# Branch tiles of the last stage loaded one by one, its first products in two halves of rows, and the sample columns split by GpSimd

## The chip, the core and the metric

The kernel runs on one core of one Trainium2 chip. The metric is the device time of one execution in microseconds (us). TensorE (PE) multiplies matrices into PSUM banks, VectorE (DVE) and ScalarE (ACT) work element by element and read the banks out, GpSimd (POOL) does a few small operations, and SyncE (SP) issues every DMA transfer from one queue, in order.

## What is computed

One layer of a decoder trunk for a prompt of 1024 rows and 32 sample rows (8 sequences of 4 tokens). The part that matters here is the merge at the end: two branches, each projected down to 1024 features, are gated, added, and go through the output projection.

```python
hc = head_rmsnorm(hc, mlstm_norm_w).reshape(B, S, MLSTM_WIDTH).astype(x.dtype)
bm = (hc * jax.nn.silu(m_z)) @ w_mlstm_down          # 2048 -> 1024
g_a, g_b = jnp.split(jax.nn.sigmoid(gate_pre), 2, axis=-1)
x = x + (g_a * a + g_b * bm) @ w_out
```

All matrix products keep fp32 accuracy by splitting both operands into a high and a low part and multiplying three times (high by high, low by high, high by low).

## The kernel before

Activations lie feature-major: 128 features on the partitions, the 1056 rows (1024 prompt, 32 sample) along the free axis. The columns are stored in two halves of 528, each with 512 prompt rows and then 16 sample rows. A product of 128 output features takes three PSUM banks of 352 columns, and for each bank 8 blocks of 128 input features, three matmuls each: 24 matmuls of 352 columns a bank. `fm` issues these for one weight slice `f`, and its consumer reads each bank out when it is full.

The order that counts runs through three pieces of `run`:

- `merge_gates` makes the two gates, 8 groups of 256 features, and stores each sigmoid tile `sz` in memory (`sgD`). Groups 0 to 5 run beside other work. Groups 6 and 7 run last, in the pool `gates3`. In the same stretch the last steps of the sample's recurrence run: loads of its state `ct`, products `num` and `kv`, and at the end the tile `hcS` (tag `ks`) with the sample's 32 columns of the mLSTM branch. PSUM holds two banks of the tag `mm` here, so the third product of a chain waits until ScalarE has read out the first.
- Between group 6 and group 7, `hc_tiles` loads the first four feature blocks of the branch (`hcD`, 512 KB each) into buffers with the tag `sz`, of which there are two, shared with the gates, and splits each into a high part (ScalarE, `mvhA`) and a low part (VectorE, `mvlA`).
- `downs` is the last stage but two. It loads blocks 4 to 7 into `mvhB`/`mvlB` (slot B1) and blocks 8 to 11 (slot B2) through two buffers `draw`, adds the sample's columns to each tile by `hc_sample` (ScalarE and VectorE), and multiplies: `half` 0 takes blocks 0 to 7, `half` 1 blocks 8 to 15. Now there are six `mm` banks. ScalarE reads the first half's banks out into `bm`; VectorE adds the second half's.

The text is written as one program, and a scheduler puts each engine's instructions in the order in which its own estimate of times has them ready. So the order on an engine is not the order of the text: it already opens six banks at once at the start of `downs` and puts the products of a late tile behind those of the tiles that are there. Each engine then works through its list strictly in order, and waits where an operand or a buffer is not ready.

In the rows, `wraw`, `whi` and `wlo` are a weight slice as loaded and its two parts. L391 to L393 are the three matmuls of `mm3`, L378 and L384 the two halves of a split without a scale, L380 and L386 those with one, L1332 the read-out of a gate bank, L1395 that of a `downs` bank, L1358 the loads of `hcD`, L1181 and L1191 loads and stores of the sample's state.

Of the kernel before, what the change touches and what calls it, by code (L numbers as in the profile page):

```python
# [10 lines left out]
F32 = mybir.dt.float32  # L11
F32R = mybir.dt.float32r
AF = mybir.ActivationFunctionType
ALU = mybir.AluOpType
# [4 lines left out]
P = 128  # L19
D = 1024  # L20
T = 1024
DB, DS = 8, 4
NS = DB * DS
NT = T + NS
# [5 lines left out]
CW = NT // 3  # L30
# [310 lines left out]
class Trunk:  # L341
# [103 lines left out]
    def fm(self, w, f, mov, consume, cw=CW):  # L445

        kt = len(w)
        for j in range(NT // cw):
            ps = self.mmps()
            for k in range(kt):  # L450
                wh, wl = w[k][:2]
                mh, ml = mov[k]
                s = slice(j * cw, (j + 1) * cw)
                self.mm3(ps[:, :cw], wh[:, f * P:(f + 1) * P], wl[:, f * P:(f + 1) * P], mh[:, s], ml[:, s],
                         k == 0, k == kt - 1)
            consume(j, ps)
        if kt == KT:
            self.tick()

    def feed(self, gen, rate):  # L460

        self.bg, self.rate, self.acc = gen, rate, 0.0
# [851 lines left out]
            for b in range(DB):  # L1314
                nc.sync.dma_start(O["new_pool_sample"][b, PH - DS:, s], st[PH + b * DS:PH + (b + 1) * DS, :])

    def merge_gates(self, groups):
        nc, I = self.nc, self.I
        for gg in groups:
            x, g = gg // 4, gg % 4  # L1320
            w = self.load_w(I["w_in"][:, O_GA + gg * 256:O_GA + (gg + 1) * 256], 256)
            for f in range(2):
                z = self.t(self.pp, [P, NT], "sz", bufs=2)

                plain = self.stats

                def ev(j, ps, z=z, plain=plain):
                    s = slice(j * CW, (j + 1) * CW)
                    if plain:
                        nc.scalar.activation(z[:, s], ps[:, :CW], AF.Copy)  # L1330
                    else:
                        nc.scalar.activation(z[:, s], ps[:, :CW], AF.Sigmoid)  # L1332
                self.fm(w, f, self.hmov, ev)
                if plain:
                    nc.scalar.activation(z, z, AF.Sigmoid)
                nc.sync.dma_start(self.sgD[x][g * 2 + f], z)


    def split(self, raw, slot, n=NT):
# [10 lines left out]

        return x.rearrange("p (a n) -> p a n", a=2)[:, :, part]

    def hc_tiles(self, pool, k0, slot, tag="draw"):

        out = []
        for k in range(k0, k0 + 4):
            raw = self.t(pool, [P, NT], tag, bufs=2)
            self.nc.sync.dma_start(self.halves(raw), self.hcD[k // 4][:, k % 4, :].rearrange("p (a n) -> p a n", a=2))  # L1358
            out.append(self.split(raw, slot, T))
        return out  # L1360

    def hc_sample(self, tiles, k0):
        for k, (hi, lo) in enumerate(tiles, k0):
            raw = self.hcS[:, k // 4, k % 4, :].rearrange("p (a n) -> p a n", a=2)
            s = slice(HT, HH)
            self.hi(self.halves(hi, s), raw)
            self.lo(self.halves(lo, s), raw, self.halves(hi, s))

    def downs(self, first):
        nc, I = self.nc, self.I  # L1370
        e = self.ep
        bm = [self.t(e, [P, NT], f"bm{f}") for f in range(KT)]
        movs = [first + self.hc_tiles(e, 4, "B1"), None]
        self.hc_sample(movs[0], 0)
        for half in range(2):
            mov = movs[half]
            if half == 0:
                movs[1] = self.hc_tiles(e, 8, "B2")
            else:
                mov += self.hc_tiles(e, 12, "B1")  # L1380
                self.hc_sample(mov, 8)
            for g in range(4):
                w = self.load_w(I["w_mlstm_down"][half * D:(half + 1) * D, g * 256:(g + 1) * 256], 256,
                                scale=self.mnw[:, half * 8:half * 8 + 8])
                for f in range(2):
                    ft = g * 2 + f
                    sb = None
                    if half:
                        sb = self.t(e, [P, NT], "sg", bufs=2)
                        nc.sync.dma_start(sb, self.sgD[1][ft])  # L1390

                    def ev(j, ps, ft=ft, half=half, sb=sb):
                        s = slice(j * CW, (j + 1) * CW)
                        if half == 0:
                            nc.scalar.activation(bm[ft][:, s], ps[:, :CW], AF.Copy)  # L1395
                            return
                        nc.vector.tensor_tensor(out=bm[ft][:, s], in0=ps[:, :CW], in1=bm[ft][:, s], op=ALU.add)
                        nc.vector.tensor_tensor(out=bm[ft][:, s], in0=bm[ft][:, s], in1=sb[:, s], op=ALU.mult)
                    self.fm(w, f, mov, ev)
        mov = []  # L1400
        for k in range(KT):
            raw = self.t(e, [P, NT], "draw", bufs=2)
            nc.sync.dma_start(raw, self.actD[k])
            mov.append(self.split(raw, "A" if k < 4 else "B2"))
        self.mmov = []
        self.ms = self.t(self.cp, [P, KT, NS], "qs")
        for g in range(4):
            w = self.load_w(I["w_pool_down"][:, g * 256:(g + 1) * 256], 256)
            for f in range(2):
                ft = g * 2 + f  # L1410
                sa = self.t(e, [P, NT], "sg", bufs=2)
                nc.sync.dma_start(sa, self.sgD[0][ft])

                def ev(j, ps, ft=ft, sa=sa):
                    s = slice(j * CW, (j + 1) * CW)
                    nc.vector.tensor_tensor(out=sa[:, s], in0=ps[:, :CW], in1=sa[:, s], op=ALU.mult)
                    nc.vector.tensor_tensor(out=bm[ft][:, s], in0=bm[ft][:, s], in1=sa[:, s], op=ALU.add)
                self.fm(w, f, mov, ev)
                nc.gpsimd.tensor_copy(self.ms[:, ft, :].rearrange("p (a n) -> p a n", a=2),
                                      self.halves(bm[ft], slice(HT, HH)))  # L1420
                self.mmov.append(self.split(bm[ft], "B1" if ft < 4 else "B2"))
# [151 lines left out]
    def run(self):  # L1573
# [80 lines left out]
        _p.close()  # L1654
        self.mpA, _ma = self.pool("movA")
        self.pp, _p = self.pool("gates3")
        self.merge_gates(range(6, 7))
        first = self.hc_tiles(self.pp, 0, "A", "sz")
        self.merge_gates(range(7, 8))
        self.drain()  # L1660
        _s[0].close()
        _p.close()
# [39 lines left out]
```

## Time and profile before

| | |
|---|---|
| time of three runs | 2196.43, 2198.58 (median), 2200.07 us |
| the profiled execution | 2201.45 us, span of the trace 2199.7 us |
| mean granted TensorE clock | 0.994 of full speed |
| PE busy | 2145.5 us, 98% of the span |
| DVE, ACT, POOL busy | 58%, 41%, 6% of the span |

Times in the trace count from the start of the span. The two groups of gates and the start of `downs` lie between about 1618 and 1712 us. A granted clock of 1.00 is 2.4 GHz, 0.50 is 1.2 GHz.

### The profile page before, as it was taken

To read this page: it belongs to the slowest core of one execution; us is meant where nothing else is said; L and a number is where in the kernel's file an instruction comes from. 1 tells how busy PE (TensorE), PEld (TensorE's weight loads), DVE (VectorE), ACT (ScalarE), POOL (GpSimd) and SP (SyncE) were. 2 spreads that over 40 slices of the span, in tenths; PEclk is the share of its full clock that TensorE was granted. 3 is DMA by queue.
4 is the path that set the end of the run, shared out by engine and by line. 5 is a ranking of instruction groups with operands and counts; after the bars stand their busy time and mean duration, and the time that the engine had idled before them with its cause. 6 is when DMAs were issued, how large, how long until landed. Compare 5 with 4: busy or idle time off the path is not lost.

```text
span 2199.7 us, 40300 instructions
## 1 busy us (share of the span) xinstructions
PE 2145.5 (98%) x16407; PEld 2051.3 (93%) x16407; DVE 1268.3 (58%) x2223; ACT 905.8 (41%) x1801; POOL 124.5 (6%) x335
## 2 busy tenths in 40 slices
PE   7999999999999999999999999999998999999998
PEld 6899999999999999899999998888888999999998
DVE  6856476556655575446566775765752243543654
ACT  5635454444544463544333443322332331213444
POOL 1200000000100010000000000000000000000000
PEclk9999999999999999999999999999999999999999
DMA  4233333333233322484655645877785242322112
GB/s 156 77 110 117 99 99 102 100 102 114 82 109 116 109 89 70 133 291 151 200 168 181 216 133 202 277 275 255 280 272 177 89 144 88 127 107 80 54 49 85
DMA packets 238858, 312.73 MB, mean 142 GB/s; under 512 B 14250, under 2 KB 170322, under 8 KB 238672
## 3 DMA queue, kind: packets, MB, share of 16 engines
q1 hardware_dynamic: 238672, 310.15, 43.5%
q8 instruction: 129, 2.11, 0.4%
q14 instruction: 57, 0.47, 0.1%
HBM read 200.01 MB, written 110.45 MB: 141 GB/s over the span
## 4 chain that ended last, share of the span: by engine, by line
PE 89%; DMA 4%; DVE 2%; ACT 2%; SPq 1%; issue 1%; POOL 0%; POOLq 0%; ACTq 0%; DVEq 0%
PE mm L221 22%; PE mm L163 15%; PE mm L391 12%; PE mm L392 12%; PE mm L393 12%; PE misc L962 2%; PE num L1183 2%; PE num L392 1%; PE num L393 1%; PE num L391 1%; PE kv L391 1%; PE kv L392 1%; PE kv L393 1%; PE kv L1187 1%; DMA ct<-state_mlstm_C 1%; PE misc L744 1%
## 5 line engine op out<-in xcount | busy, mean ns | idle before, releaser
L391 PE MATMUL mm<-hh,whi 128*128 128x352 f32 (+1 forms) x832 | 263.8, 317 | 13.1 <-ACT sz L1332 7.5
L392 PE MATMUL mm<-hl,whi 128*128 128x352 f32 (+1 forms) x832 | 262.6, 316 | 0.0
L393 PE MATMUL mm<-hh,wlo 128*128 128x352 f32 (+1 forms) x832 | 262.5, 316 | 0.0
L221 PE MATMUL mm<-wlo,hh 128*128 128x256 f32 x768 | 216.1, 281 | 0.0
L221 PE MATMUL mm<-whi,hl 128*128 128x256 f32 x768 | 216.1, 281 | 0.0
L221 PE MATMUL mm<-whi,hh 128*128 128x256 f32 x768 | 214.8, 280 | 0.0
L384 DVE TENSOR_TENSOR wlo<-wrawx,whi 128x1024 fp32r<-128x1024 f32 (+1 forms) x116 | 124.1, 1070 | 127.2 <-ACT whi L378 126.4
L391 PEld LDWEIGHTS mm<-hh,whi 128*128 128x128 f32 x832 | 158.8, 191 | 24.8 <-ACT sz L1332 8.6
L378 ACT ACTIVATE whi<-wrawx 128x1024 fp32r<-128x1024 f32 (+1 forms) x116 | 108.7, 937 | 174.8 <-PE mm L163 69.8
L378 ACT ACTIVATE whi<-wraw 128x1024 fp32r<-128x1024 f32 (+1 forms) x104 | 100.3, 965 | 174.5 <-PE mm L392 87.0
L384 DVE TENSOR_TENSOR wlo<-wraw,whi 128x1024 fp32r<-128x1024 f32 (+1 forms) x104 | 114.7, 1103 | 90.7 <-ACT whi L378 88.6
L393 PEld LDWEIGHTS mm<-hh,wlo 128*128 128x128 f32 x832 | 158.7, 191 | 8.3 <-issue 6.7
L392 PEld LDWEIGHTS mm<-hl,whi 128*128 128x128 f32 x832 | 158.7, 191 | 3.8 <-issue 2.5
L323 DVE SCALAR_TENSOR_TENSOR z<-z,vcols,z 128x556 f32<-128x556 f32 x192 | 146.4, 793 | 6.2 <-ACT z L321 4.4
L163 PE MATMUL mm<-hh,whi 128*128 128x264 f32 x512 | 148.4, 290 | 1.0 <-DVE z L179 0.6
L163 PE MATMUL mm<-hl,whi 128*128 128x264 f32 x512 | 146.1, 285 | 0.4 <-DVE hl L384 0.3
L163 PE MATMUL mm<-hh,wlo 128*128 128x264 f32 x512 | 145.5, 284 | 0.0
L221 PEld LDWEIGHTS mm<-whi,hh 128*128 128x128 f32 x768 | 144.7, 188 | 0.0
L221 PEld LDWEIGHTS mm<-whi,hl 128*128 128x128 f32 x768 | 144.6, 188 | 0.0
L221 PEld LDWEIGHTS mm<-wlo,hh 128*128 128x128 f32 x768 | 144.4, 188 | 0.2
L1188 DVE SCALAR_TENSOR_TENSOR ct<-ct,dec,kv 128x512 f32<-128x512 f32 x128 | 92.4, 744 | 85.1 <-PE kv L1187 82.5
L392 PE MATMUL mm<-mvlB,whi 128*128 128x352 f32 x384 | 123.3, 323 | 0.0
(493 smaller groups left out, 6304.3 us busy)
## 6 DMA issues: line engine op xcount, KB each, us to landing
ct<-state_mlstm_C SPq DMA_DIRECT2D x32, 1024.0 KB
new_C_sample<-ct SPq DMA_DIRECT2D x32, 1024.0 KB
wraw<-w_in SPq DMA_DIRECT2D x56, 512.0 KB
wrawx<-w_in SPq DMA_DIRECT2D x56, 512.0 KB
qkD<-z SPq DMA_DIRECT2D x64, 256.0 KB
qk<-qkD SPq DMA_DIRECT2D x16, 1024.0 KB
sgD<-sz SPq DMA_DIRECT2D x16, 528.0 KB
sg<-sgD SPq DMA_DIRECT2D x16, 528.0 KB
```

The costliest lines, as they stand in the source:

```text
L163: self.tr.nc.tensor.matmul(ps[:, j, :CH], lhsT=st[:, k], rhs=mv[k][:, c], start=start and k == 0 and n == 0, stop=stop and k == 3 and n == ...
L221: self.tr.nc.tensor.matmul(ps[:, t // 2, t % 2 * 256:t % 2 * 256 + 256], lhsT=st[k][:, c], rhs=mv[:, k], start=start and t % 2 == 0 and k ...
L323: nc.vector.scalar_tensor_tensor(out=acc, in0=z[:, o:o + tot], scalar=wc(o), in1=acc, op0=ALU.mult, op1=ALU.add)
L378: self.nc.scalar.activation(out, in_, AF.Copy)
L384: self.nc.vector.tensor_tensor(out=out, in0=in_, in1=hi.bitcast(F32), op=ALU.subtract)
L391: mm(ps, lhsT=sh, rhs=mh, start=start, stop=False)
L392: mm(ps, lhsT=sh, rhs=ml, start=False, stop=False)
L393: mm(ps, lhsT=sl, rhs=mh, start=False, stop=stop)
L744: self.nc.tensor.matmul(ps[g, f * 256:(f + 1) * 256], lhsT=self.hs[:, k, :], rhs=raw[k // 4][f][:, k % 4, :], start=k < 4, stop=k >= 4)
L962: nc.tensor.matmul(out, lhsT=qk[:, 4 + d, i * L:(i + 1) * L], rhs=qk[:, d, i * L:], start=d == 0, stop=d == 3)
L1183: nc.tensor.matmul(num[0][32 * d:32 * d + 32], lhsT=qm[:, b * P + d * NS:b * P + (d + 1) * NS], rhs=ct[:, d, :], start=b == 0, stop=b == D ...
L1188: nc.vector.scalar_tensor_tensor(out=ct[:, d, :], in0=ct[:, d, :], scalar=self.dec[:, h * DB + b, 1:2], in1=kv, op0=ALU.mult, op1=ALU.add)
```

## The change

It has four parts. `merge_gates` gets a generator to step after each gate tile and a third `sz` buffer; `hc_tiles` becomes the generator `hc_parts`, which loads a tile at each step and splits the one before it, so that the four first tiles are loaded one ahead of group 6 and one after each gate tile. In `downs` the tiles of slot B2 are loaded the same way, one step after each `fm` of the first half's groups 1 to 3. The first group of the first half goes through `fm_halves`, which opens all six banks with blocks 0 to 3 and comes back to each with blocks 4 to 7. And `hc_sample` does its two operations on GpSimd.

```diff
+    def fm_halves(self, w, mov, consume):
+
+        banks = [[self.mmps() for _ in range(3)] for _ in range(2)]
+        for k0 in (0, 4):
+            for f in range(2):
+                for j, ps in enumerate(banks[f]):
+                    s = slice(j * CW, (j + 1) * CW)
+                    for k in range(k0, k0 + 4):
+                        wh, wl = w[k][:2]
+                        mh, ml = mov[k]
+                        self.mm3(ps[:, :CW], wh[:, f * P:(f + 1) * P], wl[:, f * P:(f + 1) * P], mh[:, s], ml[:, s],
+                                 k == 0, k == 7)
+                    if k0:
+                        consume[f](j, ps)
...
-    def merge_gates(self, groups):
+    def merge_gates(self, groups, beside=None, bufs=2):
...
-                z = self.t(self.pp, [P, NT], "sz", bufs=2)
+                z = self.t(self.pp, [P, NT], "sz", bufs=bufs)
...
                 nc.sync.dma_start(self.sgD[x][g * 2 + f], z)
+                if beside is not None:
+                    next(beside)
...
+    def hc_parts(self, out, pool, k0, slot, tag="draw", bufs=2):
+
+        last = None
+        for k in range(k0, k0 + 5):
+            if last is not None:
+                out.append(self.split(last, slot, T))
+            if k == k0 + 4:
+                break
+            last = self.t(pool, [P, NT], tag, bufs=bufs)
+            self.nc.sync.dma_start(self.halves(last), self.hcD[k // 4][:, k % 4, :].rearrange("p (a n) -> p a n", a=2))
+            yield True
+        yield True
...
-            self.hi(self.halves(hi, s), raw)
-            self.lo(self.halves(lo, s), raw, self.halves(hi, s))
+            self.nc.gpsimd.tensor_copy(self.halves(hi, s), raw)
+            self.nc.gpsimd.tensor_tensor(out=self.halves(lo, s), in0=raw, in1=self.halves(hi, s).bitcast(F32),
+                                         op=ALU.subtract)
...
             if half == 0:
-                movs[1] = self.hc_tiles(e, 8, "B2")
+                movs[1] = []
+                parts = self.hc_parts(movs[1], e, 8, "B2")
...
-                    self.fm(w, f, mov, ev)
+                    if half or g:
+                        self.fm(w, f, mov, ev)
+                        if half == 0:
+                            next(parts, None)
+                    else:
+                        evs.append(ev)
+                if evs:
+                    self.fm_halves(w, mov, evs)
...
-        self.merge_gates(range(6, 7))
-        first = self.hc_tiles(self.pp, 0, "A", "sz")
-        self.merge_gates(range(7, 8))
+        first = []
+        parts = self.hc_parts(first, self.pp, 0, "A", "sz", 3)
+        next(parts)
+        self.merge_gates(range(6, 8), parts, 3)
```

Because a scheduler sets the order, the text alone does not say where an instruction ends up. Up to the last gates all engines' orders are the same. The lines of the changed text stand 15 or more further down (L1332 is L1347 there, L1358 is L1386, L1395 is L1426).

SyncE's queue in the last gates, before: `ct` is the sample's state, `sz<-hcD` are the four branch tiles, and `new_C_sample`, `sgD` are stores.

```order
L412 DMA wraw_19062<-w_mlstm_down 128x4x256
L1181 DMA ct_18652<-state_mlstm_C 128x4x512
L1191 DMA new_C_sample<-ct_18424 128x4x512
L1336 DMA sgD_44_103<-sz_18550 128x1056
L1199 DMA voz_18754<-vSD_80 128x512
L1199 DMA voz_18756<-oSD_81 128x512
L1358 DMA sz_18781<-hcD_17_76 128x2x512
...
L1336 DMA sgD_45_104<-sz_18672 128x1056
L1191 DMA new_C_sample<-ct_18652 128x4x512
L412 DMA wraw_19242<-w_mlstm_down 128x4x256
L1358 DMA sz_18793<-hcD_17_76 128x2x512
L1358 DMA sz_18799<-hcD_17_76 128x2x512
```

And in the change:

```order
L412 DMA wraw_19038<-w_mlstm_down 128x4x256
L1386 DMA sz_18538<-hcD_17_76 128x2x512
L1386 DMA sz_18678<-hcD_17_76 128x2x512
L1196 DMA ct_18654<-state_mlstm_C 128x4x512
L1206 DMA new_C_sample<-ct_18424 128x4x512
L1351 DMA sgD_44_103<-sz_18552 128x1056
L1386 DMA sz_18793<-hcD_17_76 128x2x512
...
L1351 DMA sgD_45_104<-sz_18680 128x1056
L1206 DMA new_C_sample<-ct_18654 128x4x512
L412 DMA wraw_19218<-w_mlstm_down 128x4x256
L1386 DMA sz_18891<-hcD_17_76 128x2x512
```

The first two branch tiles moved ahead of the last load of the state, and only one is left behind the last weight load, where two stood.

ScalarE's list in the last gates, before, from the second branch tile on (`voz,sss` is a step of the sample's end, `mvhA<-ks` are its columns, `sz<-mm` read-outs of gate banks):

```order
L378 ACTIVATE mvhA_18789<-sz_18787 128x2x512
L1205 ACTIVATE voz_18756,sss_18763<-shc_18761 128x512
L378 ACTIVATE mvhA_18783<-ks_18775 128x2x16
L378 ACTIVATE mvhA_18789<-ks_18775 128x2x16
L378 ACTIVATE mvhA_18795<-ks_18775 128x2x16
L378 ACTIVATE mvhA_18795<-sz_18793 128x2x512
L378 ACTIVATE mvhA_18801<-ks_18775 128x2x16
L378 ACTIVATE mvhA_18801<-sz_18799 128x2x512
L1332 ACTIVATE sz_18817<-mm_18818 128x352
L1332 ACTIVATE sz_18817<-mm_18844 128x352
L1332 ACTIVATE sz_18817<-mm_18870 128x352
```

And in the change, in the same place:

```order
L1347 ACTIVATE sz_18807<-mm_18808 128x352
L1220 ACTIVATE voz_18764,sss_18771<-shc_18769 128x512
L1347 ACTIVATE sz_18807<-mm_18834 128x352
L378 ACTIVATE mvhA_18973<-sz_18891 128x2x512
L1347 ACTIVATE sz_18807<-mm_18860 128x352
L1347 ACTIVATE sz_18893<-mm_18894 128x352
L1347 ACTIVATE sz_18893<-mm_18920 128x352
```

Two tiles and the sample's columns stood ahead of the read-out of group 7's first bank; now one tile stands ahead of its third bank, and the columns are gone from this list.

ScalarE's list at the start of `downs`, before (`draw` are the loaded tiles of slots B1 and B2, `bm<-mm` the read-outs of the six first banks):

```order
L378 ACTIVATE mvhB_2661_19012<-draw_19010 128x2x512
L378 ACTIVATE mvhB_2664_19018<-ks_18775 128x2x16
L378 ACTIVATE mvhB_2664_19018<-draw_19016 128x2x512
L380 ACTIVATE whi_19256<-wraw_19254,vcols_122 128x256 x4
L378 ACTIVATE mvhB_2667_19040<-draw_19038 128x2x512
L378 ACTIVATE mvhB_2670_19046<-ks_18775 128x2x16
L378 ACTIVATE mvhB_2670_19046<-draw_19044 128x2x512
L378 ACTIVATE mvhB_2673_19052<-ks_18775 128x2x16
L1395 ACTIVATE bm_2646_18990<-mm_19086 128x352
```

And in the change:

```order
L380 ACTIVATE whi_19232<-wraw_19230,vcols_122 128x256 x4
L378 ACTIVATE mvhB_2661_19012<-draw_19010 128x2x512
L378 ACTIVATE mvhB_2664_19018<-draw_19016 128x2x512
L378 ACTIVATE mvhB_2691_19400<-draw_19320 128x2x512
L378 ACTIVATE mvhB_2703_19508<-draw_19404 128x2x512
L1426 ACTIVATE bm_2646_18990<-mm_19062 128x352
```

The weight slice moved ahead of the third tile and the sample's columns are gone; two tiles of slot B2 still stand ahead of the first read-out.

## Rows read from the trace of the kernel before

**Rows 1.** The page's first part: busy time of each engine.
```profile
PE 2145.5 (98%) x16407; PEld 2051.3 (93%) x16407; DVE 1268.3 (58%) x2223; ACT 905.8 (41%) x1801; POOL 124.5 (6%) x335
```

**Rows 2.** Waits of PE in the whole span: us in total, times, longest us.
```profile
PE mm L391 <- ACT sz L1332: 7.5, 1, 7.5
...
PE mm L391 <- ACT bm L1395: 3.2, 1, 3.2
```

**Rows 3.** The chain that ended last, 1640 to 1725 us: start us, us, what.
```profile
1645.87 8.25 DMA sgD<-sz
...
1654.14 6.38 DMA sz<-hcD
...
1660.55 1.06 ACT mvhA L378
...
1662.18 0.66 PE mm L391
...
1666.64 0.16 PE mm L393
```

**Rows 4.** Stretches: us, busy time of each engine, granted clock, DMA share, GB/s.
```profile
1618.00:1626.00 8.00, 8.00 (x49) 7.82 (x48) 2.88 (x4) 2.94 (x4) 0.00 (x0) 1.00 0.98 309
1654.00:1662.00 8.00, 0.66 (x6) 0.40 (x4) 2.84 (x10) 3.04 (x7) 0.00 (x0) 0.85 0.54 203
1662.00:1666.00 4.00, 3.82 (x13) 3.83 (x14) 0.86 (x1) 0.48 (x2) 0.00 (x0) 0.50 0.00 0
1707.00:1711.00 4.00, 3.53 (x12) 3.53 (x13) 2.79 (x6) 4.00 (x12) 0.00 (x0) 0.57 0.61 191
```

**Rows 5.** The DMA queue SP in order of time: start us, us, transfer, count.
```profile
1626.32 0.37 SPq L1181 DMA_DIRECT2D ct<-state_mlstm_C  x1
...
1650.41 4.09 SPq L1358 DMA_DIRECT2D sz<-hcD  x2
...
1701.68 0.37 SPq L412 DMA_DIRECT2D wraw<-w_mlstm_down  x1
```

**Rows 6.** ScalarE in order of time: start us, us, operation, idle before and releaser.
```profile
1619.13 1.28 ACT L1332 ACT_TABLE_LOAD   x1 [3.12 <-DMA actD<-sz]
...
1655.03 0.47 ACT L378 ACTIVATE mvhA<-ks 128x32 fp32r<-128x32 f32 x3 [6.24 <-DVE ks L1213]
...
1702.79 1.06 ACT L378 ACTIVATE mvhB<-draw 128x1024 fp32r<-128x1024 f32 x1 [2.39 <-DMA draw<-hcD]
...
1705.89 1.06 ACT L378 ACTIVATE mvhB<-draw 128x1024 fp32r<-128x1024 f32 x1 [1.93 <-DMA draw<-hcD]
```

**Rows 7.** PE in order of time, the sample's products `num`.
```profile
1627.38 1.06 PE L1183 MATMUL num<-ct,qm 128*32 128x512 f32 x8
...
1632.92 1.05 PE L1183 MATMUL num<-ct,qm 128*32 128x512 f32 x2
...
1634.32 1.06 PE L1183 MATMUL num<-ct,qm 128*32 128x512 f32 x6
```

**Rows 8.** PE in order of time, the first products of `downs`.
```profile
1679.64 0.32 PE L391 MATMUL mm<-mvhA,whi 128*128 128x352 f32 x1
...
1703.97 0.32 PE L393 MATMUL mm<-mvhB,wlo 128*128 128x352 f32 x1
...
1707.47 0.66 PE L391 MATMUL mm<-mvhA,whi 128*128 128x352 f32 x1 [3.18 <-ACT bm L1395]
...
1711.04 0.33 PE L391 MATMUL mm<-mvhB,whi 128*128 128x352 f32 x1
```

**Rows 9.** GpSimd's copies of 32 columns: count, ns least/median/most, first and last start.
```profile
L1419 POOL COPY qs<-bm x8: 209/676/1174, 1883.5 to 1965.1; 128x32 f32<-128x32 f32 x8
```

**Rows 10.** GpSimd's operation with two inputs, of the root mean squares, columns as before.
```profile
L401 POOL TENSOR_TENSOR rs_r<-rs_ms,cst x60: 537/548/1540, 6.2 to 2195.0; 128x1 f32<-128x1 f32 x57, 32x1 f32<-32x1 f32 x3
```

**Rows 11.** GpSimd in order of time, one of the copies of 32 columns.
```profile
1895.00 1.14 POOL L1419 COPY qs<-bm 128x32 f32<-128x32 f32 x1 [11.30 <-DVE bm L1417]
```

**Rows 12.** VectorE in order of time, beside this copy.
```profile
1894.86 1.22 DVE L384 TENSOR_TENSOR wlo<-wraw,whi 128x1024 fp32r<-128x1024 f32 x1
```

More of the change, by code (lines that the diff above doesn't have):

```diff
@@ L1351, in halves, with hc_tiles @@
         return x.rearrange("p (a n) -> p a n", a=2)[:, :, part]
-    def hc_tiles(self, pool, k0, slot, tag="draw"):
+    def hc_tiles(self, pool, k0, slot, tag="draw", bufs=2):
         out = []
[L1356 to L1359, printed above, removed]
-        return out
+        for _ in self.hc_parts(out, pool, k0, slot, tag, bufs):
+            pass
+        return out
+    def hc_parts(self, out, pool, k0, slot, tag="draw", bufs=2):
[9 more added lines that the diff above has]
+        yield True
     def hc_sample(self, tiles, k0):
@@ L1384, in downs @@
                                 scale=self.mnw[:, half * 8:half * 8 + 8])
+                evs = []
                 for f in range(2):
```

## The prediction

> **What bounds the kernel now.** I read the page's first part, then the waits, the chain, the stretches, and last the engines and the DMA queue in order of time. PE is busy for 98% of the span [rows 1], so a change can only gain where PE stands, or where it runs slowly behind a stand. The list of PE's waits has two long single ones: 7.5 us for ScalarE's read-out of a gate bank and 3.2 us for its read-out of a `downs` bank [rows 2].
>
> The chain shows the first, **gap 1**, from the inside [rows 3]. The last tile of `hcD` was issued at 1654.14, when a store of a gate tile (`sgD`, 8.25 us) had given back its buffer; it took 6.38 us to land, ScalarE split it (1.06), read the bank out, and PE went on at 1662.18. PE had stood since 1662.18 − 7.5 = 1654.7. Both late tiles are in the SP row: two loads of `hcD` from 1650.41 to 1654.50 [rows 5]. The read-out itself had nothing to wait for; it stood in ScalarE's list behind these two tiles. PE then ran at a granted clock of 0.50 [rows 4], until 1666.64, where the row has a matmul of 0.16 again [rows 3]. In the stretch before the gap 49 matmuls took 8.00 us at a clock of 1.00, 0.163 each; behind it 13 took 3.82 us, 0.294 each [rows 4]. From 1662.18 to 1666.64 that makes about 15 matmuls in 4.46 us, for which 2.45 would do: **2.0 us** lost.
>
> **Gap 2** lies at the start of `downs`. PE started at 1679.64, did its last possible matmul at 1703.97 and stood until 1707.47 [rows 8], since ScalarE had two tiles of slot B2 ahead of the read-outs, which landed at 1702.79 and 1705.89 [rows 6]. Then 12 matmuls took 1711.04 − 1707.47 = 3.57 us [rows 8] at a clock of 0.57 [rows 4], for which 12 × 0.163 = 1.96 would do: 1.6 lost.
>
> **The change part by part.**
>
> *Third buffer and early loads (gap 1).* The first two tiles are now issued when the queue comes past the earlier stores, at about 1619, where ScalarE's row has a store of `actD` landing [rows 6], instead of behind the gates. The fourth needs no gate store any more; the latest it can go is where the third went, 1650.41 [rows 5]. A transfer there takes 6.38 to 8.25 us [rows 3], so it lands by 1656.8 to 1658.7, and the split ends by 1659.8. ScalarE's list now has this one tile ahead of the read-out of group 7's *third* bank only. PE stopped at 1654.7 in front of that third product; it now goes through it (24 matmuls × 0.163 = 3.9) and through the next one, and wants the bank at 1654.7 + 7.8 − 1.0 (the next part) = 1661.5. The read-out is done by about 1660.3, so 1.2 us are left at the worst. The whole 7.5 goes, and with it the cause of the slow stretch, 2.0. If the fourth tile were 3 us later than this, 2 us would come back, and the slow clock perhaps too: the low end of this part is 7.5 + 2.0 − 4.0 = 5.5.
>
> *The last load of `ct`* now stands behind two tiles. 1.05 MB at the 309 GB/s of that stretch, whose DMA share is 0.98 [rows 4], are 3.4 us. It was issued at 1626.32 [rows 5], and its products began at 1632.92: two in 1.05 us and, after a break, six in 1.06, where the eight of the step before took 1.06 together [rows 7]. In the changed PE list the eight stand in one piece and behind 18 more matmuls (18 × 0.163 = 2.9 us) and two `kv`. So the delay is covered but for about half a microsecond, and the broken turn, **1.0 us**, goes. If the load is later still, PE waits by so much, at most 3.4 when the cover fails entirely.
>
> *B2's tiles between the products (gap 2).* ScalarE still has two B2 tiles ahead of the first read-out, so the gap does not close. What moves in the queue is the weight load that was issued at 1701.68 [rows 5], between the landings of these two tiles; it now stands ahead of both. They landed 3.10 us apart [rows 6], while 512 KB at 309 GB/s take 1.7; the load in between may so have cost 1.4. Bounds: nothing, or the 1.93 us that ScalarE stood for the second tile [rows 6]. I take **1.2**, near the 1.4. About 2 us of the gap stay, and a stand of that length lies nearer to the 3.18 [rows 8] than to none, so I count no gain from the clock there (bounds 0 and 1.6).
>
> *Halves of rows.* PE's list had already opened six banks with blocks 0 to 3, so `fm_halves` writes down the order that stood there. Cost and gain 0.
>
> *Sample columns on GpSimd.* 32 small operations leave ScalarE and VectorE, which wait here for tiles, not for time; nothing gained. On GpSimd no row has this pair. The nearest are copies of 32 columns, 0.21 to 1.17 us with 0.68 in the middle [rows 9], and an operation with two inputs, 0.54 to 1.54 with 0.55 in the middle [rows 10]. A pair lies so between 0.75 and 2.71; I take 1.23, the sum of the middles. The columns are there at 1655.0 [rows 6]. The branch now starts at 1679.64 − 7.5 − 2.0 − 1.0 = 1669.1; its first bank holds no sample columns, so tiles A's four pairs are due 12 × 0.163 = 2.0 us later, at 1671.1: room for 4.0 us a pair. B1's (nine pairs in all, with one of B2 among them) are due at the earliest after six half banks, 1669.1 + 6 × 2.0 + 2.0 = 1682.8 (a little later for the last): 3.1 us a pair. Both are above the 2.71. Cost 0.
>
> One copy of 1.14 us [rows 11] lies inside a subtraction of VectorE that reads two tiles and took 1.22 [rows 12], as if it had waited for it. The Trainium skill, page "GPSIMD Engine Reference", section 8, says that GpSimd shares its SBUF interfaces with VectorE and contends with instructions of VectorE that have two SBUF inputs; this trace agrees, with 1.14 against 0.21 us. By that rule each of the two operations of a pair could wait once for such a subtraction: an estimate of 0.21 + 0.54 + 2 × 1.22 = 3.2 a pair, which would make B1 about 1 us late and the time 2188; by the rows above it costs nothing.
>
> *Sum.* −7.5 − 2.0 − 1.0 − 1.2 = −11.7. The profiled execution took 2201.45 us, 1.75 around its span of 2199.7; it lies 2.87 above the median. 2201.45 − 11.7 = 2189.75, less 2.87: **2187**.
>
> **The rivals.**
>
> *Both gaps close* (chance 0.06). If the B2 tiles land early enough, all 3.2 and the 1.6 go: −7.5 − 2.0 − 1.0 − 4.8 = −15.3, 2183.3. For it: the load of weights is out of the way. Against it: two tiles still stand ahead of the read-outs, loaded through two buffers.
>
> *A new wait takes a part back* (0.14). Behind an early tile in the queue stands `ct`, behind a late one ScalarE's third read-out. A stand of 2 to 5 us with up to 2.0 of slow clock behind it gives 2189 to 2194. For it: margins of half a microsecond and 1.2, and a queue with a share of 0.98. Against it: the 1660.3 is already worked with the longest transfer.
>
> *The change does not do what it says* (0.04): the scheduler leaves a tile ahead of the read-out that lands as late as before. Then only the 1.0 to 2 of the smaller terms are left, 2196 to 2198. Against it: the list has one tile there, and its load waits for no gate store.
>
> *GpSimd's chain becomes the bound* (0.04). Nine pairs at p us from 1655.0 on against 1682.8: late by 9p − 27.8. From p = 3.1 on PE waits, and from p = 4.9 on (16 us late) the kernel is slower than before; at 6 us a pair it would be 26 late, 2213. For it: the two-input operation takes 0.55 us for one column [rows 10], and what 32 cost is in no row. Against it: copies of 32 columns took from 0.21 us up [rows 9], so the length of a row counts little.
>
> **How the numbers follow.** The forecast as summed has 0.72, with its own range of 2184.5 to 2190 (gap 2 between nothing and 1.93, part of its slow clock, 1.5 of a smaller wait). The range takes in the closing of both gaps below and the new wait above: 2182.5 to 2194; the last two rivals, 0.08, lie outside, and a little of the others. About 0.2%, 4.4 us, is what a measurement of this kernel can tell from no change. Faster by more than that, below 2194.2: 0.72 + 0.06 + 0.09 of the new wait = 0.87. Within: the other 0.05 of it and the change without effect, 0.09. Slower: 0.04.
>
> **What the profile after would show.** If I am right: no wait of PE for the gate read-out, a clock of 1.00 through the last gates, the eight `num` in one turn, branch products from about 1669, the wait for the `downs` read-out still there at 2 to 2.5 us with a slow stretch behind it, and pairs on GpSimd of under 2.7 us. I am wrong if PE waits for `ct`, for a tile's split, or for GpSimd at a second bank, or if ScalarE's row shows a tile of `hcD` landing after 1660.

## The result, and the profile after

| | predicted | measured |
|---|---|---|
| time of the change | 2187 us (2182.5 to 2194) | 2190.78 us, median of 5 (2186.19 to 2192.16) |
| before, in the same session | | 2200.07 us, median of 5 (2196.43 to 2202.06) |
| ratio to before | 0.9947 | 0.9949, 95% interval 0.9938 to 0.9961 |

The interval says 8.6 to 13.6 us faster, 11.2 in the middle (2200.07 × 0.0051); the prediction was 11.7. The two medians of the table by themselves are 9.3 us apart, a ratio of 0.9958, near the upper end of that interval. The profiled execution took 2190.78 us, span 2189.1, which is 10.6 less than the span of before. Where these 10.6 us come from is read from the two traces between landmarks that both have.

The page of the change begins with the busy times; PE is as busy as before [rows 1], in a shorter span.

```profile
PE 2143.4 (98%) x16407; PEld 2051.0 (94%) x16407; DVE 1266.9 (58%) x2207; ACT 905.7 (41%) x1785; POOL 136.6 (6%) x367
```

In PE's waits over the whole span, the 7.5 us for the gate read-out [rows 2] has no counterpart any more. The `downs` read-out has 2.2 us where it had 3.2, and the waits for the sample's state, earlier in the kernel, have grown.

```profile
PE num L1198 <- DMA ct<-state_mlstm_C: 4.3, 6, 1.6
...
PE mm L391 <- ACT bm L1426: 2.2, 1, 2.2
```

The first landmark is the first product of gate group 6. In PE's timeline of before it stands here:

```profile
1614.76 0.33 PE L391 MATMUL mm<-hh,whi 128*128 128x352 f32 x1
```

And in the change (start, duration, line, operation) that product, the eight `num` of the last state, the first branch product, the last one before gap 2, the first behind it, and the 13th:

```profile
1617.73 0.33 PE L391 MATMUL mm<-hh,whi 128*128 128x352 f32 x1
...
1639.26 1.06 PE L1198 MATMUL num<-ct,qm 128*32 128x512 f32 x8
...
1671.64 0.32 PE L391 MATMUL mm<-mvhA,whi 128*128 128x352 f32 x1
...
1695.10 0.32 PE L393 MATMUL mm<-mvhB,wlo 128*128 128x352 f32 x1
...
1697.64 0.66 PE L391 MATMUL mm<-mvhA,whi 128*128 128x352 f32 x1 [2.22 <-ACT bm L1426]
...
1701.14 0.32 PE L391 MATMUL mm<-mvhB,whi 128*128 128x352 f32 x1
```

| stretch | before | change | difference | predicted |
|---|---|---|---|---|
| up to group 6 | 1614.76 | 1617.73 | +2.97 | 0 |
| group 6 to first branch product (gap 1) | 64.88 | 53.91 | −10.97 | −10.5 |
| first branch product to first product behind gap 2 | 27.83 | 26.00 | −1.83 | −1.2 |
| twelve matmuls behind gap 2 | 3.57 | 3.50 | −0.07 | 0 |
| from there to the end of the span | 488.66 | 487.96 | −0.70 | 0 |

The stretches that the change touches gave 12.9 us; 2.97 were lost ahead of them, in a part whose orders are the same. The waits for `ct` make 2.7 of that (4.3 here; the same line of before has 1.6 in the page of waits). How long PE stands there for the state differs from one profiled execution to the next: from 1.6 to 4.6 us over all the kernels of this document.

The stretches of the change (us, busy time of PE, PEld, DVE, ACT and POOL, granted clock, DMA share, GB/s) show that PE now has no hole and full clock where it stood and then ran at 0.50 [rows 4]; gap 2 is still followed by a clock of 0.64.

```profile
1654.00:1662.00 8.00, 8.00 (x53) 7.98 (x52) 2.97 (x6) 2.00 (x3) 2.58 (x9) 1.00 0.53 178
1662.00:1666.00 4.00, 4.00 (x27) 4.00 (x26) 0.00 (x0) 0.47 (x1) 0.00 (x0) 1.00 0.25 96
...
1694.00:1698.00 4.00, 1.78 (x10) 1.49 (x10) 1.95 (x2) 2.88 (x5) 0.00 (x0) 0.94 0.31 103
1698.00:1702.00 4.00, 4.00 (x18) 4.00 (x18) 2.33 (x6) 3.89 (x9) 0.00 (x0) 0.64 0.77 230
```

ScalarE's timeline (in brackets its idle time before, and what ended it) has the fourth branch tile at 1658.71 and right behind it the third gate bank, which waited for PE and not the other way round. PE wants that bank back when its next product is through, at 1664.20; the read-out was done at 1660.79, 3.4 us earlier. Below are the two B2 tiles and the read-outs that still queue behind them, as in [rows 6].

```profile
1658.71 1.06 ACT L378 ACTIVATE mvhA<-sz 128x1024 fp32r<-128x1024 f32 x1 [2.22 <-DMA sz<-hcD]
1660.32 0.47 ACT L1347 ACTIVATE sz<-mm 128x352 f32<-128x352 f32 x1 [0.54 <-PE mm L393]
1664.20 0.47 ACT L1347 ACTIVATE sz<-mm 128x352 f32<-128x352 f32 x1 [3.42 <-PE mm L393]
...
1694.38 1.06 ACT L378 ACTIVATE mvhB<-draw 128x1024 fp32r<-128x1024 f32 x1 [4.04 <-DMA draw<-hcD]
1696.18 1.06 ACT L378 ACTIVATE mvhB<-draw 128x1024 fp32r<-128x1024 f32 x1 [0.75 <-DMA draw<-hcD]
1697.14 1.86 ACT L1426 ACTIVATE bm<-mm 128x352 f32<-128x352 f32 x5
```

SyncE's queue of the change, to be read against [rows 5]: two tiles at 1622.7, the state 4.1 us later than before in absolute time (1.1 later when both are counted from group 6), the fourth tile at 1650.79 and the weight load ahead of the fifth and sixth `draw`.

```profile
1622.71 2.17 SPq L1386 DMA_DIRECT2D sz<-hcD  x2
1630.38 0.37 SPq L1196 DMA_DIRECT2D ct<-state_mlstm_C  x1
...
1636.86 0.36 SPq L1386 DMA_DIRECT2D sz<-hcD  x1
...
1650.79 1.34 SPq L1386 DMA_DIRECT2D sz<-hcD  x1
...
1686.39 0.37 SPq L412 DMA_DIRECT2D wraw<-w_mlstm_down  x1
```

On GpSimd a pair for the sample's columns takes 0.46 us when nothing else is about (the last two rows); the first four subtractions took 1.88 together.

```profile
1658.96 0.67 POOL L1394 CAST mvhA<-ks 128x32 fp32r<-128x32 f32 x4 [4.88 <-DVE ks L1228]
1659.59 1.88 POOL L1395 TENSOR_TENSOR mvlA<-ks,mvhA 128x32 fp32r<-128x32 f32 x4
...
1675.77 0.21 POOL L1394 CAST mvhB<-ks 128x32 fp32r<-128x32 f32 x1
1676.06 0.25 POOL L1395 TENSOR_TENSOR mvlB<-ks,mvhB 128x32 fp32r<-128x32 f32 x1
```

### The profile page after: what moved, and what is told of

It reads as the page before. It is cut to its first block, busy times and chain, and to the rows that moved or that the text cites. A ratio compares the mean times of both kernels' runs of the same rounds, so it can differ in the third digit from the quotient of the medians.

```text
span 2189.1 us, 40318 instructions
## 1 busy us (share of the span) xinstructions
PE 2143.4 (98%) x16407; PEld 2051.0 (94%) x16407; DVE 1266.9 (58%) x2207; ACT 905.7 (41%) x1785; POOL 136.6 (6%) x367
## 4 chain that ended last, share of the span: by engine, by line
PE 90%; DMA 5%; DVE 2%; ACT 1%; SPq 1%; issue 1%; POOL 0%; POOLq 0%; ACTq 0%; DVEq 0%
PE mm L221 22%; PE mm L163 15%; PE mm L391 12%; PE mm L393 12%; PE mm L392 12%; PE misc L977 2%; DMA new_C_sample<-ct 2%; PE num L392 1%; PE num L393 1%; PE num L391 1%; DMA ct<-state_mlstm_C 1%; PE kv L391 1%; PE num L1198 1%; PE kv L392 1%; PE kv L393 1%; PE misc L759 1%
```

## The experiments

Each kernel has one profile, and each ratio is to the kernel before, timed beside it. The landmarks are those of the table above: "first stretch" is group 6 to the first branch product, "restart" is the first product behind gap 2, counted from the first branch product. They say more than the times, since the lag ahead of group 6 drops out.

**One part alone, or one part undone.**

Only the sample's columns on GpSimd, in the kernel before:

```diff
-            self.hi(self.halves(hi, s), raw)
-            self.lo(self.halves(lo, s), raw, self.halves(hi, s))
+            self.nc.gpsimd.tensor_copy(self.halves(hi, s), raw)
+            self.nc.gpsimd.tensor_tensor(out=self.halves(lo, s), in0=raw, in1=self.halves(hi, s).bitcast(F32),
+                                         op=ALU.subtract)
```

> The kernel before with only the sample's columns split by GpSimd. Theory (the gain is the third buffer and the early loads): ScalarE's list still has the third and fourth tile of hcD ahead of the read-out of group 7's first bank, so the stand of 7.5 us and the slow stretch behind it stay, and the time is that of before, ratio 0.999 to 1.001; the stretch from the first gate matmul of group 6 to the first branch matmul stays at 64 to 65 us (64.9 before, 53.9 in the change). Rival (the columns held up ScalarE's list, which stood for them until 1655): the stand shrinks by some 3 us or more, ratio 0.9985 or less.

Measured: ratio 0.9996 (0.9987 to 1.0005), first stretch 66.06 us, restart 27.95. In PE's waits gap 1 is all there:

```profile
PE mm L391 <- ACT sz L1332: 8.1, 1, 8.1
```

The rival falls: the columns stood in ScalarE's list, but it was the two tiles behind them that PE waited for.

Only the early loads (the change with `hc_tiles(e, 8, "B2")`, `fm` for all groups, and the columns on ScalarE and VectorE):

```diff
+        first = []
+        parts = self.hc_parts(first, self.pp, 0, "A", "sz", 3)
+        next(parts)
+        self.merge_gates(range(6, 8), parts, 3)
```

> The change with only its first part: third buffer and tiles of hcD loaded one by one; tiles of slot B2 loaded together, no halves, columns on ScalarE and VectorE. Theory: the first stretch takes 53.9 us, plus at most 1 for the four columns that ScalarE splits ahead of a read-out; about 10 us faster than before, ratio 0.9952 to 0.996, and the gap at the start of the last stage stays near 3 us. Rival (the parts only work together): the columns, which come late, hold up ScalarE ahead of the read-out of the third bank, PE stands there for 2 us or more, and the ratio is 0.997 or more.

Measured: ratio 0.9954 (0.9941 to 0.9966), first stretch 53.90, restart 27.98. The theory holds: the first part alone gives the whole of gap 1, and nothing of gap 2.

The change without GpSimd (the first diff turned round):

> The change with the sample's columns left on ScalarE and VectorE. Theory: these engines have room, and the time is that of the change: ratio 0.994 to 0.996 to before, first stretch 53.9 to 55. Rival (the columns on GpSimd free ScalarE where it counts): 1 to 3 us slower than the change, with a new wait of PE for ScalarE in the last gates.

Measured: 0.9950 (0.9937 to 0.9964), first stretch 53.90, restart 26.58. As the theory has it; GpSimd's part is worth nothing that can be seen.

The change with two `sz` buffers:

```diff
-        parts = self.hc_parts(first, self.pp, 0, "A", "sz", 3)
+        parts = self.hc_parts(first, self.pp, 0, "A", "sz", 2)
...
-        self.merge_gates(range(6, 8), parts, 3)
+        self.merge_gates(range(6, 8), parts, 2)
```

> The whole change, but with two buffers for gate tiles and branch tiles instead of three. Theory: the order of ScalarE is nearly the same, yet the second and third tile wait again for a gate store to give back its buffer (8.25 us in a row of before), and the third now stands ahead of the read-out of group 7's first bank: PE stands there 1 to 5 us, some of the slow clock comes back, and the gain falls to about half, ratio 0.996 to 0.999. Rival (the early place in the program is what counts, the third buffer nothing): same as the change, ratio 0.995.

Measured: 0.9950 (0.9938 to 0.9963), first stretch 53.93, restart 26.70. Here **my theory falls**, and the time is as the rival has it. ScalarE's timeline has the fourth tile, the third bank and the fourth:

```profile
1660.36 1.06 ACT L378 ACTIVATE mvhA<-sz 128x1024 fp32r<-128x1024 f32 x1 [2.61 <-DMA sz<-hcD]
1661.57 0.47 ACT L1347 ACTIVATE sz<-mm 128x352 f32<-128x352 f32 x1 [0.15 <-PE mm L393]
1665.41 0.47 ACT L1347 ACTIVATE sz<-mm 128x352 f32<-128x352 f32 x1 [3.38 <-PE mm L393]
```

Counted from the first product of group 6, the fourth tile comes 0.4 us later than in the change (41.40 against 40.98). The read-out is done at 1662.04 and wanted at 1665.41, 3.4 us later, as in the change. The third buffer buys nothing.

The change with the tiles stepped later:

```diff
-        next(parts)
-        self.merge_gates(range(6, 8), parts, 3)
+        self.merge_gates(range(6, 7), None, 3)
+        next(parts)
+        next(parts)
+        self.merge_gates(range(7, 8), parts, 3)
+        next(parts)
```

> The change with its branch tiles stepped later: the first two loads behind group 6, where they stood before, the third and fourth behind the two gate tiles of group 7; all else as in the change. Theory (what counts is that no late tile stands ahead of a gate read-out, not that the loads are early): the order of ScalarE has the third tile ahead of the third bank only, the first stretch is 54 to 56 us, ratio 0.994 to 0.996. Rival (the early loads count): the third and fourth tile land late, and PE waits for them at the start of the branch or for a read-out behind them by 4 us or more, ratio 0.997 or more.

Measured: 0.9951 (0.9936 to 0.9965), first stretch 55.63, restart 26.20. ScalarE's rows for the third and fourth tile, and PE's for `num`:

```profile
1662.46 1.06 ACT L378 ACTIVATE mvhA<-sz 128x1024 fp32r<-128x1024 f32 x1 [3.26 <-DMA sz<-hcD]
...
1668.37 1.06 ACT L378 ACTIVATE mvhA<-sz 128x1024 fp32r<-128x1024 f32 x1 [0.95 <-DMA sz<-hcD]
```

```profile
1637.39 1.05 PE L1198 MATMUL num<-ct,qm 128*32 128x512 f32 x2 [0.40 <-DMA ct<-state_mlstm_C]
...
1638.79 1.06 PE L1198 MATMUL num<-ct,qm 128*32 128x512 f32 x6
```

The fourth tile is split later than in the kernel before, 49.6 us behind group 6's first product (at 1618.75 here) against 45.8 [rows 3], and PE stands for none of them: there is no wait for a read-out or a tile in the first stretch. The third was split 43.7 us behind that product, against 44.5 before. So the early loads are not what closed gap 1. What did is that one late tile stands ahead of group 7's *third* bank in ScalarE's list, and no longer two ahead of its first. The 1.7 us that this kernel is longer lie with `num`, which here breaks into two and six again and waits 0.40 for the state: the small term of the sum, by itself. That much the early steps do give.

**Gap 2.** The change with B2's tiles loaded together:

```diff
-                movs[1] = []
-                parts = self.hc_parts(movs[1], e, 8, "B2")
+                movs[1] = self.hc_tiles(e, 8, "B2")
```

> The change with slot B2's tiles loaded all four together as before; early loads, halves and GpSimd as in the change. Theory (the 1.8 us that gap 2 lost come from the weight load that now stands ahead of two B2 tiles; here it stands there too): PE starts again 26.0 to 26.7 us after the first branch matmul, as in the change, and the ratio is 0.994 to 0.996. Rival (the gain in gap 2 comes from B2's tiles one by one): 27.8 us as before, 1 to 2 us slower than the change.

Measured: 0.9949 (0.9935 to 0.9963), restart 26.51, as the theory has it.

The change without the halves:

```diff
-                    if half or g:
-                        self.fm(w, f, mov, ev)
-                        if half == 0:
-                            next(parts, None)
-                    else:
-                        evs.append(ev)
-                if evs:
-                    self.fm_halves(w, mov, evs)
+                    self.fm(w, f, mov, ev)
+                    if half == 0 and g:
+                        next(parts, None)
```

> The change with the first group of the last stage in whole chains again, block 0 to 7 bank by bank as written (no halves of rows); all else as in the change. Theory (the halves, not the tiles of B2 one by one, are what moved the weight load ahead of two B2 tiles: in this kernel's queue it stands behind them again): PE starts again 27.8 to 28.1 us after the first branch matmul, 1.5 to 2 us later than in the change, ratio 0.995 to 0.9965. Rival (the 1.8 us come from B2's tiles one by one): 26.0 to 26.7 as in the change, ratio 0.994 to 0.9955.

Measured: 0.9943 (0.9931 to 0.9955), first stretch 53.92, restart 26.28. SyncE's weight load, ScalarE's split of the sixth `draw` tile, and PE's restart:

```profile
1690.86 0.37 SPq L412 DMA_DIRECT2D wraw<-w_mlstm_down  x1
```

```profile
1694.02 1.06 ACT L378 ACTIVATE mvhB<-draw 128x1024 fp32r<-128x1024 f32 x1 [0.96 <-DMA draw<-hcD]
```

```profile
1695.48 0.45 PE L391 MATMUL mm<-mvhA,whi 128*128 128x352 f32 x1 [2.04 <-ACT bm L1426]
```

The weight load stands behind the sixth tile in this kernel, at 1690.86, and the gap is as short as in the change. The theory fails for it, and the time is as the rival has it; but the rival's cause, B2's tiles one by one, is not shown either, since the kernel above has them together and restarts at 26.51.

The direct test, on the kernel with only the early loads:

```diff
-            nc.sync.dma_start(raw[:, :kk, :n], ap[k0 * P:(k0 + kk) * P].rearrange("(k p) n -> p k n", p=P))
+            cut = short and k0 == 4
+            kl = 1 if cut else kk
+            nc.sync.dma_start(raw[:, :kl, :n], ap[k0 * P:(k0 + kl) * P].rearrange("(k p) n -> p k n", p=P))
```

> The kernel with only the early loads of the first part, and one weight load cut from 512 to 128 KB: the load that is issued right behind the second tile of slot B2, in the first half's third group (its input blocks 5 to 7 then use the weights of block 4, so the output differs from the reference). All orders and all work of the engines stay. In the same kernel with the whole load, the sixth draw tile was split 26.40 us after the first branch matmul and PE started again at 27.98. Theory (that load shares the queue with the sixth tile and delays it): the tile is split at 24.6 to 25.4, PE starts again at 26.0 to 26.8. Rival (the landing varies by itself, or by what else goes on, the load does nothing): 26.0 to 26.6, and 27.6 to 28.1.

Measured: 0.9945 (0.9929 to 0.9962); the sixth tile was split at 25.74, and PE started again at 27.32:

```profile
1694.61 1.06 ACT L378 ACTIVATE mvhB<-draw 128x1024 fp32r<-128x1024 f32 x1 [1.78 <-DMA draw<-hcD]
```

```profile
1696.19 0.66 PE L391 MATMUL mm<-mvhA,whi 128*128 128x352 f32 x1 [3.10 <-ACT bm L1427]
```

That is neither forecast. With three quarters of the load gone, 0.66 us came back, one profile against one, of the 1.4 that I had put down to it.

Four `draw` buffers, in the change (B1's, B2's and the later tiles alike):

```diff
-        movs = [first + self.hc_tiles(e, 4, "B1"), None]
+        movs = [first + self.hc_tiles(e, 4, "B1", bufs=4), None]
...
-                parts = self.hc_parts(movs[1], e, 8, "B2")
+                parts = self.hc_parts(movs[1], e, 8, "B2", bufs=4)
```

> The change with four buffers draw instead of two in the last stages. Theory (gap 2 is two B2 tiles that land late, because they wait for two buffers): all four tiles of B1 are issued at once and those of B2 4 to 7 us earlier, ScalarE's list has one tile of B2 ahead of the first read-out, the wait of 2.2 us goes below 0.5 and with it the slow stretch (1.6): 3 to 4 us faster than the change, ratio to before 0.9925 to 0.994. Rival (the queue is full, tiles land no earlier, since B1's loads now share it): the wait stays at 1.5 us or more, ratio 0.9945 to 0.9955.

Measured: 2186.22 us, ratio 0.9924 (0.9910 to 0.9938). ScalarE's rows around the first read-out, and the stretches of this kernel:

```profile
1690.74 1.06 ACT L378 ACTIVATE mvhB<-draw 128x1024 fp32r<-128x1024 f32 x1 [2.67 <-DMA draw<-hcD]
1691.71 0.80 ACT L1426 ACTIVATE bm<-mm 128x352 f32<-128x352 f32 x2
```

```profile
1690.00:1694.00 4.00, 4.00 (x27) 4.00 (x26) 1.73 (x2) 3.25 (x6) 0.00 (x0) 1.00 1.03 361
1694.00:1698.00 4.00, 4.00 (x27) 4.00 (x26) 3.86 (x5) 4.00 (x9) 0.00 (x0) 1.00 0.81 241
```

One B2 tile stands ahead of the first read-out and comes 3.6 us before the place where the change has its first (1694.38). Gap 2 and its slow clock are gone: 27 matmuls in 4 us where the change has 10 and then 18. From group 6 to the end of the span this kernel takes 567.4 us, the change 571.4. No kernel here is faster; the times of the next one can't be told from these.

The buffers did two things at once: the tiles land earlier, and the list has one of them ahead of the first read-out where it had two. No run parts these. The rows say that either would nearly do. The second B2 tile's split begins at 1692.40 here, so even with both ahead the read-outs would have begun at 1693.5, and PE stood from 1695.4 in the change. And with the change's landings, one tile ahead ends at 1695.4, where PE would stand by about half a microsecond: an estimate from the rows above, as it goes on 0.5 us after the first read-out starts (1697.64 and 1697.14).

Four `draw` buffers with only the early loads:

```diff
-        movs = [first + self.hc_tiles(e, 4, "B1"), None]
+        movs = [first + self.hc_tiles(e, 4, "B1", bufs=4), None]
...
-                movs[1] = self.hc_tiles(e, 8, "B2")
+                movs[1] = self.hc_tiles(e, 8, "B2", bufs=4)
```

> Only the early loads of the first part and four draw buffers; no halves, B2's tiles loaded together, columns on ScalarE and VectorE. Theory (these two things are the whole gain): as the change with four buffers, ratio 0.9915 to 0.994, first stretch 53.9, no wait for the first read-outs of the last stage. Rival (halves, GpSimd or B2's parts are needed once the tiles are early): 1.5 us or more slower, with a wait of PE for a tile or a read-out in the last stage's first 30 us.

Measured: 2185.55 us, 0.9928 (0.9914 to 0.9942), first stretch 53.90, 568.2 us from group 6 to the end of the span, no wait for a read-out; PE waited 0.2 us for one tile. So two edits, the tiles stepped between the gates and the buffers, are the whole of what these edits gain; halves, GpSimd and B2's parts add nothing to them that can be seen.

The same edit in the kernel before:

> The kernel before with four draw buffers only. Theory (the two gaps are independent): gap 1 stays at 7 to 8 us, gap 2 and its slow stretch go, 4 to 5 us faster than before, ratio 0.9975 to 0.9985. Rival (without the early loads the queue is too full for four draws at once): no change, 0.999 or more.

Measured: 0.9975 (0.9964 to 0.9986). Gap 2 is closed, and gap 1 stands, a little shorter than the 7 to 8 us that I had expected:

```profile
PE mm L391 <- ACT sz L1332: 6.1, 1, 6.1
```

The two gaps are independent as far as the ratios can tell: 0.9949 and 0.9975 multiply to 0.9924, which is what both edits together measured.

**The rival on the other side.** GpSimd's operations ten times over:

```diff
-            self.nc.gpsimd.tensor_copy(self.halves(hi, s), raw)
-            self.nc.gpsimd.tensor_tensor(out=self.halves(lo, s), in0=raw, in1=self.halves(hi, s).bitcast(F32),
-                                         op=ALU.subtract)
+            for _ in range(10):
+                self.nc.gpsimd.tensor_copy(self.halves(hi, s), raw)
+            for _ in range(10):
+                self.nc.gpsimd.tensor_tensor(out=self.halves(lo, s), in0=raw, in1=self.halves(hi, s).bitcast(F32),
+                                             op=ALU.subtract)
```

> The change with each of GpSimd's two operations on the sample's columns done ten times over, same values, 640 small operations. A pair took 0.46 to 0.64 us in the change, so it takes 4.6 or more here. Theory by the formula of the prediction: with the columns there 2.7 us after the place of before, nine pairs end 14 us after B1's are due, PE waits for GpSimd by about 14 us, ratio to before 1.000 to 1.003. Rival (the scheduler knows how long GpSimd takes and moves the products of those columns behind others on PE): 3 to 8 us slower than the change at most, ratio 0.996 to 0.999.

Measured: 0.9991 (0.9981 to 1.0000), some 9 us slower than the change (0.9991 − 0.9949, of 2200): between the two forecasts, nearer to the rival's 8. In GpSimd's groups of this kernel (busy us, mean ns) the eight pairs of the `mvhB` tiles, ten copies and ten subtractions each, are busy for 20.7 + 20.5 us, 5.2 us a pair (the mean lengths add up to 5.7, but one operation starts before the one ahead of it has ended). PE's list of waits in the last stage has GpSimd in it, where that of the change has the `downs` read-out alone:

```profile
L1395 POOL CAST mvhB<-ks 128x32 fp32r<-128x32 f32 x80 | 20.7, 290 | 2.2 <-PE mm L393 2.2
L1397 POOL TENSOR_TENSOR mvlB<-ks,mvhB 128x32 fp32r<-128x32 f32 x80 | 20.5, 278 | 0.1
```

```profile
PE mm L392 <- POOL mvlA L1397: 2.2, 1, 2.2
```

The mechanism is as the rival had it, and its size is short of the formula's. The waits that name GpSimd come to 5.0 us, the 2.2 here and 2.8 in four waits of the second half. Slow clock is a part of the rest: between 1690 and 1700 PE's granted clock is 0.83 (0.87 in the change), and in the ten us before it is 0.89 where the change has 1.00.

```profile
1690.00:1700.00 10.00, 6.99 (x31) 6.20 (x30) 4.55 (x6) 3.29 (x5) 10.00 (x37) 0.83 0.67 210
```

How the 9 us divide beyond that is not shown. PE's order differs from the change's: behind the first products with tiles A come two banks' worth with tiles B1, and then tiles A again for a new bank, where the change goes through six banks with tiles B1 in a row. That fits the rival, as two of the six banks hold no sample columns: the scheduler put the products with sample columns behind others, so less of the chain showed than the formula has with a fixed order.

## Why the prediction was right, and where it was not

**Gap 1, 7.5 + 2.0 + 1.0.** Size and place were right: 10.97 for 10.5, no stand, full clock, `num` in one turn. The step on the cause was half wrong. I argued from the third buffer, which frees the fourth tile from a gate store, and from the early loads. With two buffers the stretch is the same to 0.02 us, and with loads as late as before there is no stand either. What all three share is ScalarE's list, one tile ahead of the third bank. I had that in the sum as well (the bank is wanted at 1661.5 and not at 1654.7), but took it for a margin; it was enough by itself. No run has the early tiles with the old list; an estimate from the rows says that they would not have been enough: the fourth tile's split ended 42.0 us behind group 6's first product (1659.77 against 1617.73), and before, PE stood from 39.9 (1654.7 against 1614.76). The margin itself came out at 3.4 us, not 1.2, since I had let the fourth tile land as late as any row allowed.

**`num`.** The 1.0 was about right for the broken turn; the kernel with late tiles shows 1.7 with a wait for the state of 0.40 in it, which leaves 1.3.

**Gap 2, −1.2.** The gap stayed, as forecast, at 2.2 us and with its slow stretch. The term measured −1.83, inside the bounds of 0 and 1.93 that went with it. The cause that I gave, a weight load between the two tiles, is borne out only in part, so that the size came out inside its bounds is in part luck; what shortened the gap is not settled. Restart was at 27.83 to 27.98 in three kernels with the weight load behind the sixth tile, at 26.0 to 26.7 in five with it ahead, but at 26.28 in one with it behind; and cutting the load to a quarter gave 0.66. Each is one profiled execution, and the split of the sixth tile begins between 24.5 and 26.5 us over all of them. How much of this range is the weight load and how much other traffic stays open. That four buffers in place of two close the gap is shown, in three kernels.

**Halves, B2's parts, GpSimd: 0.** Right: each left out alone gives 0.9943 to 0.9950, against 0.9949 with all of them. The 2.71 us that I had as the upper bound of a pair was far off; 0.46 is the usual one.

**The rivals.** Both gaps closing needed another edit. The new wait did not come: 3.4 us of margin stood at ScalarE where I had seen 1.2. GpSimd's chain turns most of the gain back at 5.2 us a pair, near the 4.9 where the formula has all of it gone; the formula's lateness, 14 us at 4.6 a pair, was too large, with some 9 measured.

**The whole.** For the profiled execution I had 2189.75. The stretches of the change, −12.9, give 2188.6; the lag of 2.97 ahead of them, which I had at 0, less the 0.70 behind them, took it to 2190.8. The range should have carried a term for what differs between executions: the five times of the change alone span 6 us.

## What to carry to other kernels

When an engine that works strictly in order stands, look first at which late operand is ahead of the wanted instruction in its list, and move that by one place; here the further buffer gave nothing beyond that, and the earlier loads only the 1.7 us at `num`. A gap behind two loads through two buffers closed here with more buffers, and not with a finer order of the loads that left both ahead of the wanted read-out; moving one of them behind it, with two buffers, was not tried. Where a gain of some 0.5% is split over several stretches, measure it between landmarks of the trace: the waits for the state ahead of them differed by up to 3 us between the executions here.

## What the hardware showed beyond that

The slow clock came behind each stand for a `downs` read-out, down to one of 1.78 us (the kernel with GpSimd times ten, in the stretch above with its clock of 0.83). In all eleven kernels that stood so, matmuls 0.29 us apart, as at the granted clock of 0.50 in [rows 4], followed within the next dozen, in three of them not before the seventh. I had counted no gain there, and that held.

The four subtractions on GpSimd from 1659.59 to 1661.47, 1.88 us for what took 0.88 in the kernel with two `sz` buffers, where no operation of VectorE runs beside them, lie beside this subtraction of VectorE with two inputs:

```profile
1659.81 1.32 DVE L384 TENSOR_TENSOR mvlA<-sz,mvhA 128x1024 fp32r<-128x1024 f32 x1 [0.38 <-ACT mvhA L378]
```

The Trainium skill, page "GPSIMD Engine Reference", section 8, has this contention with VectorE's instructions that read two SBUF inputs. The trace agrees: the extra 1.00 us is a wait once for the four of them, since the first two took 0.47 together and the other two 1.45. The kernel with GpSimd times ten shows the same beside another subtraction of VectorE; two copies take 0.35 there when they run alone:

```profile
1694.36 1.35 DVE L384 TENSOR_TENSOR mvlB<-draw,mvhB 128x1024 fp32r<-128x1024 f32 x1 [2.38 <-ACT mvhB L378]
```

```profile
1694.53 1.40 POOL L1395 CAST mvhB<-ks 128x32 fp32r<-128x32 f32 x2
```

The estimate of 3.2 us a pair, which lets each operation wait, was far too high: in the change GpSimd's chain for the first half met only one such subtraction of 1024 columns, and a pair beside shorter ones took at most about 0.8.
